# The products of the sample states with R~ | A~ made among the second layer's last gates, with their results in the sample's operand slots

## The chip, the cores and the metric

The kernel runs on one core of one Trainium2 chip. The metric is device time in microseconds (us) of one execution, the median of several runs. The engines of the core are TensorE (PE, with its weight loads as PEld), VectorE (DVE), ScalarE (ACT), GpSimd (POOL) and SyncE (SP, which issues most of the DMA transfers).

## The reference, cut to what matters

Two layers of a decoder trunk run over 1024 prompt tokens and over 8 sample sequences of 8 tokens each, 1088 tokens in all. Layer 0 mixes tokens with HGRN2, layer 1 with RWKV-7. Only layer 1 is touched. Its recurrence, for each of 16 heads of width 64, is

```
def step(S, inp):
    r_t, w_t, k_t, v_t, a_t, b_t = inp
    sa = jnp.einsum('bhij,bhj->bhi', S, a_t)
    S = S * w_t[:, :, None, :] + sa[..., None] * b_t[:, :, None, :] + v_t[..., None] * k_t[:, :, None, :]
    y = jnp.einsum('bhij,bhj->bhi', S, r_t)
    return S, y
```

The prompt starts from a zero state. Each of the 8 sample sequences starts from a state of its own, `state_rwkv` (8 x 16 x 64 x 64). Beside the mixer the layer has memory cross-attention and a gate of 1536 columns: the branch is multiplied by SiLU(gate) and projected back.

## The kernel before

Layer 1 is computed in blocks (class `Blk`): 8 of 128 prompt tokens and one, the sample block, of the 64 sample tokens; they run in the order of `RSEQ`, block 0, the sample block, block 1, 2 and so on. For a block, `pre` makes the decayed operands R~ and A~ (tile `AR`) and K~ and B~ (`BKz`); `score_steps` multiplies them to the matrix `Q` (products `psc`); `tokens` transposes `BKz` (`pbk`, `BKt`); `inverse` makes the inverses of the small triangular parts, mostly 30 short instructions on DVE, one after the other (`pd`, `Xc`), between `Ld`, `Lu` and `XN`, `XP`; `merge_steps` puts them together by many products of 32 x 32 on PE (`pn`, `px`, `py`). `chain` is the recurrence: PSUM tiles `chain0`, `chain1` and `chainS` begin with what the incoming state contributes, the first product by `Q` goes to `W` (ACT), the second to `UV` (DVE), the third gives the outputs `yv`.

For a prompt block, the incoming state is one matrix for all tokens. For the sample block it is 8 matrices for a pair of heads, and `sample_in` (line 1606) makes the product of each with its sequence's part of `AR`. It runs 8 times: for one pair of heads, 4 DMAs on SP bring the state (`Sn0`, rows of 256 bytes), PE transposes it into PSUM (line 1602, `ps`), ACT copies it out (`S0T`), PE makes 8 products for each of two heads (line 1617, `pas`, 16 columns each), and ACT copies each head's result into `AS0`. All of `ps` and `pas` go through one PSUM buffer (`psn`). `chain` of the sample block then adds `AS0` into `chain0` and `chain1` by products with the identity (line 1647). The sample block's chain comes second; `sample_in` stands ahead of the chain of the first (`SIN = 0`).

Ahead of the chains stand 12 gates. `gate(n)` loads 128 weight columns, multiplies them in three pieces of columns (384, 384, 320) with all 1088 tokens, 24 products a piece (72 rows of PE a gate, lines 216 to 218, into PSUM tiles `pg`), evacuates each piece by a DVE instruction (line 157), three ACT instructions (158 to 160) and a DVE product (line 1136), and sends the 544 KB of the gate (`evs`) to memory (`gT`). The three `pg` buffers hold the three pieces of one gate; the 5 slots of the ring `evslot` are given out in the order of the program. `PLAN` and `PLAN2` (line 43) set that order: cross-attention heads (x), the sample's cross-attention (s, products `pss`, `ppts`, `pos`, `pots`), gates (g) and the parts of the first two blocks. After `PLAN`, the PSUM of the cross-attention (`psx`) is closed and `psn` is opened in its place.

Within the order of the pools, a scheduler places each engine's instructions by times of its own. So the queues of the engines, which run in that order on the chip, are read from the built program.

Of the kernel before, what the change touches and what calls it, by code (L numbers as in the profile page):

```python
# [9 lines left out]
F32 = mybir.dt.float32  # L10
F32R = mybir.dt.float32r
I32 = mybir.dt.int32
AF = mybir.ActivationFunctionType
# [7 lines left out]
NB = 8  # L21
LS = 8
# [18 lines left out]

PARTS = dict(p="pre", c="score", t="tokens", i="inverse", m="merge")
PLAN, PLAN2 = [[(x[0], int(x[1:])) for x in l.split()] for l in (
    "x0 g0 x1 x2 g1 x3 g2 s0 g3 s1 g4 p0 c0 s2 g5 s3", "t0 i0 m0 p1 g6 g7 g8 g9 g10 g11")]
SIN = 0
EM = "sss"
ENG = dict(wm="gpsimd", um="gpsimd", vb="gpsimd", om="gpsimd", oa="gpsimd", bk0="gpsimd", bk1="vector", arA="gpsimd", arR="gpsimd", bx="vector", de="vector", ys="gpsimd", yr="vector", arC="gpsimd", sm="gpsimd", sa="vector", snm="vector", sna="vector", bkt="scalar", xm="scalar", ye="scalar")
# [925 lines left out]
def rwkv_layer(ctx, g, nn, left):  # L973
    nc, tc = g.nc, g.tc
# [70 lines left out]
    with pool(g, "lora", LB, "right") as lp:  # L1045
# [29 lines left out]
        for t0, n in PCS:  # L1075
# [3 lines left out]
            ps, pq = (g.psg.tile([128, 512], F32, name="pg", tag="g") for _ in range(2))  # L1079
            m = min(n, TP - t0)  # L1080
            smp = m < n
            for z, (wh, wl) in enumerate(l1):
                o, w = (pq, m) if z else (ps, n)
                for k in range(KT):
                    ks, x = slice(128 * k, 128 * k + 128), slice(t0, t0 + w)
                    for i, (a, v) in enumerate(((wh, xh), (wh, xl), (wl, xh))):
                        nc.tensor.matmul(o[:, :w], a[:, ks], v(k)[:, x], start=k + i == 0,
                                         stop=(k, i) == (KT - 1, 2) and (z == 1 or not smp))
# [98 lines left out]
    def gate(j, gemm=gemm_cm):  # L1187
        proj(3584, [j], xh, xl, g.gT, "silu", gemm=gemm, raws=1)
# [35 lines left out]
    for kind, n in PLAN2:  # L1224
        if kind == "g":
            gate(n)
        else:
            ops(n, PARTS[kind])
    es.close()

    with pool(g, "rl", 1, "right") as rl, pool(g, "sm2", 2, "right") as g.sm2:
# [19 lines left out]
        ops(2, "pre")  # L1251
        pairs = list(range(8))
        for n, x in enumerate(seq):
            if n == SIN:
                smp.sample_in()
            with tc.high_priority():
                x.chain()
            ops(n + 1, "values")
            weave(seq[n + 1].merge_steps() if n + 1 < len(seq) else (), seq[n + 2].score_steps() if n + 2 < len(seq) else (), *WV)
            ops(n + 2, "tokens", "inverse")  # L1260
            ops(n + 3, "pre")
            if n:
                seq[n - 1].out()
            if n > seq.index(smp) and pairs:
                smp.sample_out(pairs[:SOUT])
                pairs = pairs[SOUT:]
            if n == len(seq) - 2:
                pS.close()
                g.wp = ctx.enter_context(pool(g, "wp2", 2))
                owa, orb = ctx.enter_context(pool(g, "owA", 1)), ctx.enter_context(pool(g, "orb1", 1))  # L1270
                first = BranchTile(g, 1, orb, SEQ[0])
                first.load(KS)
                ws = load_out_w(g, 1, owa, [(g.wp, {})], KS[:OWB])
# [91 lines left out]
class Blk:  # L1365
# [22 lines left out]

    def pre(self):

        self.AR, self.ec = [], []
        for k in range(2):
            self.pre_group(k)

    def pre_group(self, k):
# [11 lines left out]
        k2 = ld(g.k2T, "k2")  # L1407
        a = self.at % 3
        AR = self.spare("AR", f"{('xhi', 'xlo')[k]}{4 + a}", 1024)
        AR = AR.rearrange("p (c e t) -> p c e t", c=4, t=64)  # L1410
        self.AR.append(AR)
        BK = g.BKz[k]
# [175 lines left out]
        for _ in self.merge_steps():  # L1588
            pass

    def sample_state(self, p):

        g = self.g
        nc = g.nc
        S0T = self.tile("S0T", "S0T", NB, 64)
        ps = g.psn.tile([128, NB, 64], F32, name="ps0", tag="n")
        for b0 in range(0, NB, 4):
            Sn0 = self.tile("Sn0", "Sn0", 4, 2, 64, p=64)
            for h in range(2):
                nc.sync.dma_start(out=Sn0[:, :, h, :], in_=g.state_rwkv[0, b0:b0 + 4, 2 * p + h].rearrange("b i j -> i b j"))  # L1600
            for bb in range(4):
                nc.tensor.transpose(ps[:, b0 + bb, :], Sn0[:, bb].rearrange("p h j -> p (h j)"), g.ident[:64, :64])
        nc.scalar.activation(S0T, ps, AF.Copy)
        return S0T

    def sample_in(self):

        g = self.g
        nc = g.nc
        self.AS0 = self.tile("AS0", "AS0", 4, 2, 128)  # L1610
        for p in range(8):
            S0T = self.sample_state(p)
            o = HV[p // 4]
            for h in range(2):
                ps = g.psn.tile([128, 2, NB, LS], F32, name="pas", tag="n")
                for bb in range(NB):
                    nc.tensor.matmul(ps[o, :, bb, :], S0T[HV[h], bb, :], self.AR[p // 4][HV[h], p % 4, :2, LS * bb:LS * bb + LS],  # L1617
                                     start=True, stop=True)
                nc.scalar.activation(self.AS0[o, p % 4, h], ps[o].rearrange("p a b t -> p (a b t)"), AF.Copy)

    def chain(self):

# [9 lines left out]
        for e in range(E):  # L1632
# [7 lines left out]
            def start(k):  # L1640
                G = Gs[k]
                if not self.sample and not S:
                    nc.tensor.matmul(G, g.zb, g.zb[:, None, :].to_broadcast([128, 4, 128]), start=True, stop=False)
                for j in range(4):
                    if self.sample:
                        for h in range(2):
                            nc.tensor.matmul(G[:, j, HV[h]], self.AS0[HV[k], j, h], g.ident[HV[k], HV[k]],
                                             start=j + h == 0, stop=False)
                    elif S:
                        nc.tensor.matmul(G[:, j], AR[k][:, j, 2 * e:2 * e + 2].rearrange("p a t -> p (a t)"), S[k][:, j],  # L1650
                                         start=j == 0, stop=False)
# [201 lines left out]
```

## Time and profile before

| | |
|---|---|
| runs of the kernel before | 2386.75, 2386.9, 2400.98 us |
| median | 2386.9 us |
| the profiled execution's own time | 2401.76 us |
| its span | 2399.8 us |
| PE busy | 2238.2 us (93%), 20980 instructions |
| DVE, ACT, POOL busy | 1332.2, 1004.3, 717.7 us |
| mean granted clock of PE | 0.934 of full speed |

The profiled execution is one like the slowest of the three runs. Times within it are counted from the span's start. The first layer and the projections of the second fill the span to about 1500 us, the cross-attention and the gates to 1745, the chains to about 2205, the output projection the rest. A line of a view names the engine, the line of the code, the result and its operands, the count, and in brackets how long the engine stood idle before, and what ended that.

### The profile page before, as it was taken

What the parts mean: (1) busy time and instruction counts of PE and PEld (TensorE: products, weight loads), DVE (VectorE), ACT (ScalarE), POOL (GpSimd) and SP (SyncE); (2) the same over time, 40 slices, a digit from 0 to 9 for tenths busy, and PEclk for the clock granted to TensorE, in tenths of its full rate; (3) what the DMA queues carried; (4) which work ended last, traced back from release to release, by engine and by line L of the source; (5) the groups of instructions that cost most, each with busy time, mean ns of one, the idle gap of its engine ahead of it and who ended that gap; (6) DMA issues with size and microseconds to landing.
All of it is one profiled execution on the core that took longest, in us unless ns stands there. A gap on an engine that the chain in (4) does not pass through costs nothing. (4 is left out here: it accounts for less than half of the span.)

```text
span 2399.8 us, 50625 instructions
## 1 busy us (share of the span) xinstructions
PE 2238.2 (93%) x20980; PEld 2001.5 (83%) x20981; DVE 1332.2 (56%) x2678; ACT 1004.3 (42%) x2240; POOL 717.7 (30%) x559
## 2 busy tenths in 40 slices
PE   5988999999999979989989998999999998899997
PEld 5988888888788858878979998898889987788786
DVE  6113566556775553365796214245576589874643
ACT  4222444444444442266554313344544455444421
POOL 2123121122112310034553412113143255444432
PEclk9998999999999989999999998999986798887999
DMA  5334111223432264215434425145332233312653
GB/s 184 86 96 142 48 56 45 67 70 91 111 87 87 80 193 127 84 41 199 148 122 163 127 93 145 50 103 134 113 108 72 57 101 99 90 55 82 201 158 105
DMA packets 360312, 252.99 MB, mean 105 GB/s; under 512 B 120379, under 2 KB 326403, under 8 KB 360083
## 3 DMA queue, kind: packets, MB, share of 16 engines
q1 hardware_dynamic: 348034, 237.66, 33.3%
q0 software_dynamic: 2544, 7.64, 0.9%
q10 hardware_dynamic: 9504, 4.46, 0.7%
q8 instruction: 165, 2.70, 0.5%
q14 instruction: 65, 0.52, 0.1%
HBM read 172.59 MB, written 77.11 MB: 104 GB/s over the span
## 5 line engine op out<-in xcount | busy, mean ns | idle before, releaser
L200 POOL TENSOR_TENSOR wlo<-wraw,whi 128x1024 fp32r<-128x1024 f32 (+1 forms) x84 | 214.9, 2560 | 646.5 <-ACT whi L197 623.8
L216 PE MATMUL pg<-hi,whi 128*128 128x288 f32 (+3 forms) x800 | 269.1, 336 | 4.5 <-DVE qk L597 2.3
L218 PE MATMUL pg<-hi,wlo 128*128 128x288 f32 (+3 forms) x800 | 266.0, 333 | 0.0
L217 PE MATMUL pg<-lo,whi 128*128 128x288 f32 (+3 forms) x800 | 265.9, 332 | 0.0
L197 ACT ACTIVATE whi<-wraw 128x1024 fp32r<-128x1024 f32 (+1 forms) x92 | 101.0, 1099 | 178.5 <-issue 104.9
L216 PEld LDWEIGHTS pg<-hi,whi 128*128 128x128 f32 x800 | 153.8, 192 | 21.5 <-issue 4.4
L217 PEld LDWEIGHTS pg<-lo,whi 128*128 128x128 f32 x800 | 153.7, 192 | 12.9 <-issue 3.1
L218 PEld LDWEIGHTS pg<-hi,wlo 128*128 128x128 f32 x800 | 153.5, 192 | 11.8 <-issue 2.3
L890 PE MATMUL pout<-owh,bh 128*128 128x512 f32 (+1 forms) x432 | 143.1, 397 | 9.2 <-ACT owh L197 9.2
L890 PE MATMUL pout<-owl,bh 128*128 128x512 f32 (+1 forms) x432 | 142.0, 394 | 0.1
L890 PE MATMUL pout<-owh,bl 128*128 128x512 f32 (+1 forms) x432 | 141.2, 394 | 0.9 <-DVE bl L200 0.9
L216 PE MATMUL pg<-xhi,whi 128*128 128x384 f32 (+2 forms) x392 | 127.6, 325 | 7.1 <-DVE evs L1136 5.0
L218 PE MATMUL pg<-xhi,wlo 128*128 128x384 f32 (+2 forms) x392 | 126.4, 322 | 0.0
L217 PE MATMUL pg<-xlo,whi 128*128 128x384 f32 (+2 forms) x392 | 125.5, 320 | 0.0
L1461 PE MATMUL psc<-AR,BKz 128*128 128x128 f32 x544 | 98.2, 342 | 17.2 <-DVE Q L1464 9.3
L1461 PEld LDWEIGHTS psc<-AR,BKz 128*128 128x128 f32 x544 | 86.7, 244 | 23.1 <-DVE Q L1464 11.0
L890 PEld LDWEIGHTS pout<-owh,bh 128*128 128x128 f32 (+1 forms) x432 | 78.9, 183 | 31.3 <-ACT owh L197 10.8
L197 ACT ACTIVATE bh<-br 128x512 fp32r<-128x512 f32 (+1 forms) x54 | 32.4, 606 | 171.5 <-POOL br L859 84.4
L200 DVE TENSOR_TENSOR bl<-br,bh 128x512 fp32r<-128x512 f32 (+1 forms) x54 | 49.6, 919 | 96.2 <-ACT bh L197 96.2
L890 PEld LDWEIGHTS pout<-owh,bl 128*128 128x128 f32 (+1 forms) x432 | 78.6, 182 | 22.8 <-DVE bl L200 1.8
L242 PE MATMUL pg<-xhi,wlo 128*128 128x384 f32 (+1 forms) x408 | 96.6, 334 | 0.0
L890 PEld LDWEIGHTS pout<-owl,bh 128*128 128x128 f32 (+1 forms) x432 | 78.8, 183 | 21.1 <-DVE owl L200 0.6
(460 smaller groups left out, 6114.9 us busy)
## 6 DMA issues: line engine op xcount, KB each, us to landing
wraw<-in_w_in_dram SPq DMA_DIRECT2D x72, 512.0 KB
oraw<-in_w_out_dram SPq DMA_DIRECT2D x24, 512.0 KB
wraw<-in_w_mem_kv_dram SPq DMA_DIRECT2D x16, 512.0 KB
gT<-evs SPq DMA_DIRECT2D x12, 544.0 KB
vv<-vtk SPq DMA_DIRECT2D x24, 256.0 KB
br<-brT SPq DMA_DIRECT2D x24, 256.0 KB
br<-mixT SPq DMA_DIRECT2D x24, 256.0 KB
gt<-gT SPq DMA_DIRECT2D x24, 256.0 KB
```

The source lines that it names most:

```text
L197: nc.scalar.activation(hi, src, AF.Copy)
L200: (nc.gpsimd if elo == "pool" else nc.vector).tensor_sub(lo, src, hi.bitcast(F32))
L216: nc.tensor.matmul(out, ah, bh, start=first, stop=False)
L217: nc.tensor.matmul(out, ah, bl, start=False, stop=False)
L218: nc.tensor.matmul(out, al, bh, start=False, stop=last)
L242: nc.tensor.matmul(z[:, :n], a[:, k], x(k)[:, t0:t0 + n], start=first, stop=last)
L890: nc.tensor.matmul(ps[c][:p], a[:, k, :p], w[:, 512 * c:512 * c + 512], start=first, stop=last)
L1461: nc.tensor.matmul(ps[:, j], two(BK[:, h, j, 2 * e:2 * e + 2]), two(AR[:, j, 2 * e:2 * e + 2]), start=True, stop=True)
```

## The change

`sample_in` and `sample_state` take one pair of heads as an argument and are no longer called ahead of the first chain. `PLAN2` gets eight items a0 to a7, two behind each of the gates 6 to 9, which call them. The state and its transpose (`Sn0`, `S0T`) take slots of `evslot`, and the results go into the upper halves of the two spare slots in which the sample's `AR` uses the lower halves only. Nothing is computed otherwise.

```diff
 PLAN, PLAN2 = [[(x[0], int(x[1:])) for x in l.split()] for l in (
-    "x0 g0 x1 x2 g1 x3 g2 s0 g3 s1 g4 p0 c0 s2 g5 s3", "t0 i0 m0 p1 g6 g7 g8 g9 g10 g11")]
+    "x0 g0 x1 x2 g1 x3 g2 s0 g3 s1 g4 p0 c0 s2 g5 s3", "t0 i0 m0 p1 g6 a0 a1 g7 a2 a3 g8 a4 a5 g9 a6 a7 g10 g11")]
...
     for kind, n in PLAN2:
         if kind == "g":
             gate(n)
+        elif kind == "a":
+            smp.sample_in(n, evslot)
...
         for n, x in enumerate(seq):
-            if n == SIN:
-                smp.sample_in()
             with tc.high_priority():
                 x.chain()
...
         AR = self.spare("AR", f"{('xhi', 'xlo')[k]}{4 + a}", 1024)
+        if self.sample:
+
+            self.AS0.append(AR[:, 512:].rearrange("p (c h t) -> p c h t", c=2, h=2))
+            AR = AR[:, :512]
...
-    def sample_state(self, p):
+    def sample_state(self, p, slot_):
...
-        S0T = self.tile("S0T", "S0T", NB, 64)
+        S0T = slot_("S0T")[:, :512].rearrange("p (b i) -> p b i", b=NB)
+        Sn = slot_("Sn0")[:64, :1024].rearrange("p (a b h j) -> p a b h j", a=2, b=4, h=2)
...
-            Sn0 = self.tile("Sn0", "Sn0", 4, 2, 64, p=64)
+            Sn0 = Sn[:, b0 // 4]
...
-    def sample_in(self):
+    def sample_in(self, p, slot_):
...
-            nc.scalar.activation(self.AS0[o, p % 4, h], ps[o].rearrange("p a b t -> p (a b t)"), AF.Copy)
+            nc.scalar.activation(self.AS0[j // 2][o, j % 2, h], ps[o].rearrange("p a b t -> p (a b t)"), AF.Copy)
...
-                            nc.tensor.matmul(G[:, j, HV[h]], self.AS0[HV[k], j, h], g.ident[HV[k], HV[k]],
+                            nc.tensor.matmul(G[:, j, HV[h]], self.AS0[j // 2][HV[k], j % 2, h], g.ident[HV[k], HV[k]],
```

Lines behind the changed ones stand 2 to 4 lines further down (157, 216 to 218 and 1136 keep theirs; 1602 is 1607 now, 1617 is 1620, 1619 is 1622, 1652 is 1655).

The first place is PE at the end of the sample's cross-attention, around its last two softmaxes. Before:

```order
L216 MATMUL pg<-xhi,whi 128x384
L217 MATMUL pg<-xlo,whi 128x384
L425 MATMUL pots<-ident,oS 128x128
L218 MATMUL pg<-xhi,wlo 128x384
L216 MATMUL pg<-xhi,whi 128x384
L217 MATMUL pg<-xlo,whi 128x384
```

Of the change (the gate row at its end is the first of gate 8; 288 gate rows are still to come there):

```order
L415 MATMUL pos<-xlo,PTs 32x128 x16
L402 MATMUL pss<-kcT,qs 32x256 x8
L408 MATMUL ppts<-ident,prob 128x128 x4
L415 MATMUL pos<-xlo,PTs 32x128 x16
L425 MATMUL pots<-ident,oS 128x128
L1607 MATMUL ps_17672<-ident,Sn_17671 128x64 x8
L1620 MATMUL pas<-AR,S0T 64x2x8 x8
L1493 MATMUL pbk<-ident,BKz_15166 128x64 x16
L1620 MATMUL pas<-AR,S0T 64x2x8 x8
L1465 MATMUL psc<-AR,BKz_15165 128x128 x8
L1607 MATMUL ps_17708<-ident,Sn_17707 128x64 x8
L1620 MATMUL pas<-AR,S0T 64x2x8 x8
```

Before, gate rows stand between all the steps of the cross-attention and behind it: at `pots` 190 of the rows of gates 6 to 11 are still to come. Now none stand between the last `pss` and gate 8, and 98 more are left for later.

The second place is DVE, where gate 7 is evacuated. Its three pieces are `pg_17677`, `pg_17707` and `pg_17737` before, ahead of the last softmax:

```order
L157 TENSOR_SCALAR evs_17676<-pg_17677 128x384
L326 TENSOR_SCALAR nm_16926<-mx_16924 128x2
L332 RECIPROCAL ri_16931<-smx_16928 128x2
L334 TENSOR_TENSOR ri_16931<-ri_16931,bmask_122 128x2
L336 TENSOR_SCALAR prob_16923<-prob_16923,ri_16931 128x256 x2
L1136 TENSOR_TENSOR evs_17676<-pg_17677,evs_17676 128x384
L157 TENSOR_SCALAR evs_17676<-pg_17707 128x384
L1136 TENSOR_TENSOR evs_17676<-pg_17707,evs_17676 128x384
L157 TENSOR_SCALAR evs_17676<-pg_17737 128x320
L1136 TENSOR_TENSOR evs_17676<-pg_17737,evs_17676 128x320
```

They are `pg_17749`, `pg_17779` and `pg_17809` with the change:

```order
L1538 TENSOR_TENSOR pd_17227<-Xc_15171,L16_17225 128x14x14
L157 TENSOR_SCALAR evs_17748<-pg_17749 128x384
L1539 TENSOR_REDUCE Xc_15171<-pd_17227 128x14
L157 TENSOR_SCALAR evs_17748<-pg_17779 128x384
L157 TENSOR_SCALAR evs_17748<-pg_17809 128x320
L1538 TENSOR_TENSOR pd_17227<-Xc_15171,L16_17225 128x15x15
L1539 TENSOR_REDUCE Xc_15171<-pd_17227 128x15
L1136 TENSOR_TENSOR evs_17748<-pg_17749,evs_17748 128x384
L1545 STREAM_TRANSPOSE XN_17261<-XI_17258 128x16x2x16
L1546 STREAM_TRANSPOSE XP_17262<-XI_17258 128x16x2x16
L1136 TENSOR_TENSOR evs_17748<-pg_17779,evs_17748 128x384
L1136 TENSOR_TENSOR evs_17748<-pg_17809,evs_17748 128x320
```

Gate 7's evacuation now stands in the last steps of block 0's inverse; until then its pieces hold all three `pg` buffers.

The third place is ACT, at the evacuation of gates that run behind block 0's merge. Before, a piece's three instructions (here of gate 11) follow each other:

```order
L158 ACTIVATE evs_18068<-evs_18068 128x384
L159 ACTIVATE evs_18068<-evs_18068 128x384
L160 ACTIVATE evs_18068<-evs_18068 128x384
L1295 ACTIVATE XM_17265<-px32_17338 32x512
L1295 ACTIVATE XM_17265<-px32_17339 32x512
L158 ACTIVATE evs_18068<-evs_18068 128x384
```

With the change (gate 9, and the copies of a4 and a5):

```order
L1608 ACTIVATE S0T_18010<-ps0_18012 128x512
L1622 ACTIVATE AR_17532<-pas_18026 64x128
L1622 ACTIVATE AR_17532<-pas_18036 64x128
L197 ACTIVATE whi_18350<-wraw_18352 128x1024
L1608 ACTIVATE S0T_18046<-ps0_18048 128x512
L158 ACTIVATE evs_18088<-evs_18088 128x384 x2
L159 ACTIVATE evs_18088<-evs_18088 128x384
L158 ACTIVATE evs_18088<-evs_18088 128x320
L1622 ACTIVATE AR_17532<-pas_18062 64x128
L159 ACTIVATE evs_18088<-evs_18088 128x384
L160 ACTIVATE evs_18088<-evs_18088 128x384
```

All of gate 9's sigmoids now stand behind a5's copy `S0T_18046`, whose source PE makes only behind the last row of gate 9.

## Rows read from the trace of the kernel before

**Rows 1.** The page, part 2: clock of PE in 40 slices, tenths
```profile
PEclk9998999999999989999999998999986798887999
```

**Rows 2.** Windows: stretch, length, busy PE, PEld, DVE, ACT, POOL (count); clock, DMA
```profile
1755.00:1790.00 35.00, 32.59 (x432) 30.11 (x432) 31.62 (x60) 14.27 (x33) 19.35 (x22) 0.94 0.41 111
1790.00:1832.00 42.00, 42.00 (x424) 39.24 (x423) 25.50 (x54) 17.94 (x43) 14.65 (x11) 0.52 0.24 64
1832.00:1846.00 14.00, 14.00 (x255) 13.05 (x254) 9.92 (x13) 9.80 (x25) 3.39 (x3) 0.93 0.31 76
1846.00:1894.00 48.00, 48.00 (x552) 45.08 (x551) 20.22 (x46) 17.52 (x42) 6.96 (x6) 0.50 0.25 62
```

**Rows 3.** Timeline of PE: start, duration, engine, line, tiles, count [idle before]
```profile
1678.21 1.08 PE L415 MATMUL pos<-xlo,PTs 128*32 128x128 f32 x32
...
1710.23 0.69 PE L216 MATMUL pg<-xhi,whi 128*128 128x384 f32 x1 [3.54 <-DVE evs L1136]
...
1723.62 1.20 PE L1560 MATMUL pn<-XN,Q 32*32 32x32 f32 x64
...
1751.13 3.78 PE L1461 MATMUL psc<-AR,BKz 128*128 128x128 f32 x16
...
1754.85 2.15 PE L1652 MATMUL chain<-UV,Q 128*64 128x64 f32 x32
```

**Rows 4.** Tile windows of PE: `pas`, then `ps`: length, busy (rows), clock, DMA
```profile
1754.00:1790.00 36.00, 4.58 (x64) 0.93 0.42 113
1790.00:1890.00 100.00, 21.05 (x192) 0.57 0.24 62
...
1754.00:1790.00 36.00, 2.69 (x24) 0.93 0.42 113
1790.00:1890.00 100.00, 4.83 (x42) 0.57 0.24 62
```

**Rows 5.** Timeline of DVE, from the last softmax to the inverse's end
```profile
1680.22 0.69 DVE L324 TENSOR_REDUCE mx<-pss 128x2 f32<-128x512 f32 x1 [0.57 <-PE pss L402]
...
1683.15 0.62 DVE L336 TENSOR_SCALAR prob<-prob,ri 128x256 f32<-128x256 f32 x2
...
1696.28 0.28 DVE L426 COPY os<-pots 128x128 f32<-128x128 f32 x1
...
1700.58 0.70 DVE L1528 STREAM_TRANSPOSE Lu<-Ld 128x512 f32<-128x512 f32 x1
...
1720.47 1.12 DVE L1541 STREAM_TRANSPOSE XN<-XI 128x512 f32<-128x512 f32 x1 [0.52 <-ACT XI L1538]
```

**Rows 6.** Source view of `Ld`: ns min/median/max, first and last start
```profile
L1525 ACT ACTIVATE Ld<-Q,bm x16: 483/510/532, 1692.8 to 1698.9; 32x128 f32<-32x128 f32 x16
```

**Rows 7.** Groups of DVE, 1700 to 1723 us: count | busy, mean ns | idle before
```profile
L1534 DVE TENSOR_TENSOR pd<-Xc,L 128x1 f32<-128x1 f32 (+14 forms) x15 | 5.4, 361 | 0.4
L1535 DVE TENSOR_REDUCE Xc<-pd 128x1 f32<-128x1 f32 (+14 forms) x15 | 3.6, 239 | 0.4
L1415 DVE TENSOR_TENSOR_SCAN G<-smask,sg 128x512 f32<-128x512 bf16 x1 | 3.3, 3326 | 0.0
L157 DVE TENSOR_SCALAR evs<-pg 128x384 f32<-128x384 f32 (+1 forms) x4 | 2.1, 532 | 5.0 <-PE pg L218 5.0
...
L1425 DVE TENSOR_TENSOR BKz<-bb,sg 64x256 f32<-64x256 f32 x2 | 1.4, 702 | 0.0
```

**Rows 8.** Tile window of PE: gate rows, length, busy (rows), clock
```profile
1676.00:1706.00 30.00, 24.64 (x145) 1.00 0.45 135
```

**Rows 9.** ACT: a group of the gates' sigmoids, 1676 to 1755; the first `S0T`
```profile
L158 ACT ACTIVATE evs<-evs 128x384 f32<-128x384 f32 (+1 forms) x13 | 6.5, 501 | 18.6 <-DVE evs L157 18.6
...
1759.13 0.60 ACT L1603 ACTIVATE S0T<-ps 128x512 f32<-128x512 f32 x1
```

**Rows 10.** Timelines of SP and DVE behind the last gate row
```profile
1744.52 0.32 SPq L1141 DMA_DIRECT2D gT<-evs  x1
...
1747.92 1.29 DVE L1464 TENSOR_TENSOR Q<-psc,rms 128x512 f32<-128x512 f32 x2 [3.43 <-DMA UV<-vtk]
```

More of the change, by code (lines that the diff above doesn't have):

```diff
@@ L1389, in pre @@
     def pre(self):
-        self.AR, self.ec = [], []
+        self.AR, self.ec, self.AS0 = [], [], []
         for k in range(2):
@@ L1604, in sample_state @@
         return S0T
-    def sample_in(self):
+    def sample_in(self, p, slot_):
         g = self.g
         nc = g.nc
[L1610 to L1618, printed above, removed]
-                nc.scalar.activation(self.AS0[o, p % 4, h], ps[o].rearrange("p a b t -> p (a b t)"), AF.Copy)
+        S0T = self.sample_state(p, slot_)
+        o, j = HV[p // 4], p % 4
+        for h in range(2):
+            ps = g.psn.tile([128, 2, NB, LS], F32, name="pas", tag="n")
+            for bb in range(NB):
+                nc.tensor.matmul(ps[o, :, bb, :], S0T[HV[h], bb, :], self.AR[p // 4][HV[h], j, :2, LS * bb:LS * bb + LS],
+                                 start=True, stop=True)
+            nc.scalar.activation(self.AS0[j // 2][o, j % 2, h], ps[o].rearrange("p a b t -> p (a b t)"), AF.Copy)
     def chain(self):
```

## The prediction

> **What bounds the kernel now.** I read the page first, for PE's clock: it is nearly full everywhere but in two or three slices around 1800 to 1900 us, where the chains begin [rows 1]. The windows then split that stage. From 1755 to 1790 DVE is busy 31.62 of 35 us and PE 32.59, both nearly full at a clock of 0.94. From 1790 to 1894 PE has no idle time at all (42.00 of 42, 14.00 of 14, 48.00 of 48), and 90 of these 104 us run at about 0.5, which is the 1.2 GHz level [rows 2]. So there PE alone is the bound, and any row taken from it shortens the stage. `pas` and `ps` belong to that stage: 4.58 + 2.69 us of them lie before 1790, 21.05 + 4.83 us behind it [rows 4].
>
> Ahead of it, the timelines of PE and DVE and the source view of `Ld` give a string of dependences: last softmax, last `os`, `Ld`, `Lu`, the inverse on DVE, `XN`, the merge (`pn`), the first `chain` product at 1754.85 [rows 3, 5, 6]. In the kernel before, PE fills the waits of this string with gate rows, 145 of them between 1676 and 1706 at 24.64/145 = 0.17 us a row [rows 8]. The one visible wait of a gate row is 3.54 us at 1710.23, for gate 7's evacuation [rows 3].
>
> **What is removed.** Nothing is computed less. The rows of `pas` and `ps` leave the chain stage. Behind 1790 they are 21.05 + 4.83 = 25.9 us of a busy PE: I count all of it as gained there. Before 1790 I count nothing of the 7.27 us, since DVE's 31.62 of 35 us stays; the bounds are 0 and 3.4 us, DVE's idle share. The copies on ACT leave too (0.60 us for an `S0T` [rows 9]); ACT is busy 14.27 of 35 there [rows 2], so they are worth nothing.
>
> **What is added among the gates.** At full clock a `pas` row costs 4.58/64 = 0.072 us and a `ps` row 2.69/24 = 0.112 us [rows 4], so the 256 and 66 rows are 18.3 + 7.4 = 25.7 us. If they only lengthened PE's work there, the change would exchange 25.9 for 25.7. What decides is therefore whether PE has waits there that they fill, or whether new waits come. I follow the string.
>
> *The last softmax.* Thirteen gate rows less stand ahead of the second-last `pos`, 13 x 0.17 = 2.2 us, so the last `mx` comes at 1678.0 for 1680.22. From `mx` to the end of `prob` it is 3.6 us [rows 5]; the transposes, `pos` (1.08 us [rows 3]), `pots` and `os` (0.28 [rows 5]) take some 3.4 more with no gate row in between. `os` is done at about 1685 for 1696.56: 11.5 us earlier, but PE stands idle for about 4.6 us of it, which the gates filled.
>
> *The inverse.* The 16 `Ld` take 6.6 us from 1692.8 to 1699.4 [rows 6]; `Lu` moves from 1700.58 to about 1691. From `Lu` to `XN` it was 19.9 us [rows 5]. What DVE must do in it: `pd` 5.4, `Xc` 3.6, the scan `G` 3.3, `BKz` 1.4, three of gate 7's L157 1.6, `Lu` 0.7 [rows 5, 7], together 16.0, and about 3.3 of small instructions and gaps. That is 19.3, so `XN` comes at about 1710.3 for 1720.47. In this stretch PE has only a0, a1, `pbk` and the first `psc`: gate 8's first row waits until gate 7's first L1136 has been done, and that stands behind the last `Xc`. So PE is idle from about 1697 to 1709, 11 or 12 us. This is the new wait, and its counterpart before was 3.54 us.
>
> *The merge.* `pn` came 3.15 us behind `XN`, and the first `chain` 3.7 us behind the `psc` at 1751.13 that closes the stretch [rows 3]. So `pn` is at 1713.4 for 1723.62. From `pn` to that `psc` it was 27.5 us; with fewer gate rows but a2 and a3 in between I take 28.5, to 1741.9.
>
> *What is left then.* Before, the last gate row had run by this time. Now the 216 rows of gates 9 to 11 are left, 216 x 0.17 = 36.7 us, and a4 to a7, half of the sample's rows: 9.2 + 3.6 = 12.8 us. Together, to 1791.4. On ACT, the sigmoids of gates 9 and 10 stand behind `S0T` of a5 and a7, whose source PE makes only behind the gate's last row; so the `pg` buffers come free late, and the first row of gates 10 and 11 waits for a `S0T`, three ACT instructions (0.501 us each [rows 9]) and DVE's two. The trace has no such wait. Below it is 0 (if the sigmoids' times allow the three buffers to turn), above 6 us, two pieces' evacuations; the nearest row is the 3.54 us [rows 3], and I take 3.2 each: 1797.8.
>
> *The last gate.* Behind its last row come an L157 (0.53), three of ACT (1.5), an L1136 (0.5), the `gT` transfer, and then the load of `UV` from the memory side: from the issue at 1744.52 to the `Q` that waited for it at 1747.92 are 3.4 us [rows 7, 9, 10]. That is 6.1 us during which PE has nothing, since all else of the two blocks is done. Before, 3.78 us of `psc` and parts of the merge covered it [rows 3]. The first `chain` starts at about 1803.9 for 1754.85: **49 us later**.
>
> **The sum.** 49 - 25.9 = +23 us against the profiled execution's own 2401.76, so 2425. That execution lies 14.9 us above the median, 2386.9, and no row says where the shorter runs gain; the likeliest place is the stretch at half clock, the only large part of the trace whose length could change with no instruction changed. There, less of the 25.9 us would be saved. A version whose PE idles so often before the chains will not lack half-clock stretches either. I take half of the 14.9: **2417 us**, +1.3% against the median. About 1% (24 us) is what a measurement of this kernel can tell from no change.
>
> **The rivals.**
> 1. *The forecast*: the wait before gate 8, the late gates and the lost cover of the last evacuation outweigh the gain, the clock stays as it is: 2408 to 2432. Chance 0.45.
> 2. *The clock*: the stage runs at full clock once the sample's small rows have left it. Its 100 us of PE behind 1790 become 45 to 50, DVE's 25.50 + 9.92 + most of 20.22 us [rows 2] then set about 58. That is -42 for -25.9, so +7 against the profile, 2409, or 2395 to 2412. For it: ahead of the first fall, around 1790, PE is not full (32.59 of 35). Against it: at 1846 the clock falls with PE busy 14.00 of 14 and 48.00 of 48 on the two sides [rows 2]. Chance 0.18. The Trainium skill (TensorE: Matmul & The Clock Gate, Part 1: The HAM clock gate) says that the throttled clock is the default, that sustained activity of PE releases it and idleness brings it back; by this rule a stage without idle time would be at the full level. The trace disagrees: PE is busy 48.00 of 48.00 us at 0.50 [rows 2], so the rule gets this smaller chance.
> 3. *The stalls are half as long*: DVE reaches gate 7's L1136 earlier, or the `S0T` don't hold the sigmoids. 6 us less before gate 8 and 6 us less at gates 10 and 11 give a chain start of +37 and a sum of +11 on the profile; against the median with shorter half-clock stretches, 2388 to 2404. Chance 0.15.
> 4. *The other side*: the inverse, now 10 us earlier, is done before PE runs out of work, and the sample's rows take the place of the 3.54 us wait. Then the chain starts only 25.7 - 3.5 = 22 us later, and with rival 2's stage (-42) the time is 20 us below: 2367 to 2382 as profile or run goes. It decides itself at gate 8's first row: PE idle under 3 us there and `pn` by 1705. Against it: DVE's 19.3 us of its own work between `Lu` and `XN`. Chance 0.09.
> 5. *Worse*: the idle stretches bring half the clock into the first 35 us of the chains too. PE's 32.59 - 7.27 = 25.3 us there become about 48, 13 more than the 35: 2430 to 2440. The waits for the last gate, 6.1 us with nothing for PE just ahead of the chains, speak for it. Chance 0.13.
>
> **How the numbers follow.** 2417 is the first case. The range leaves out 4 and the upper half of 5, some 0.15: 2388 to 2434. Faster by over 1% means under 2363: only the tail of 4, 0.03. Slower by over 1%, above 2411: seven eighths of the first case, all of 5 and the tip of 2, 0.54. The rest, 0.43 (2 and 3, most of 4, an eighth of the first), is within 1%.
>
> **What would show it.** In the profile after: PE idle some 4 to 5 us around 1686 and some 11 us before gate 8's first row, which waits for DVE's `evs` of L1136; `XN` near 1710 and `pn` near 1713; waits of about 3 us for ACT or DVE at the first rows of gates 10 and 11; 72 rows of gate 11 alone, about 6 us of idle PE, and the first `chain` near 1804; no `pas` behind it; the stretch between there and block 1's chain shorter by about 26 us, at half clock again. I would be wrong if PE's idle time before gate 8 is small, if the gates' rows run under the inverse after all, or if the chain stage's clock is full or much worse: the last moves the time by 17 to 40 us and no order of instructions shows it.

## The result and the profile after

The changed kernel takes 2423.4 us (median of 4 runs, 2420.4 to 2431.2) against 2393.3 us for the kernel before (4 runs, 2386.8 to 2401.0): a ratio of 1.013, interval 1.0082 to 1.0177, so about 30 us slower. In the runs of the experiments below the kernel before had a median of 2393 to 2395, with single runs from 2380 to 2407. The profiled execution of the change took 2422.14 us, near its median; that of before was one of the longer runs (2401.76).

To compare the two traces, one row serves as a mark: the last transpose of the cross-attention's heads (`ppt`), ahead of everything that the change moves. The source view gives for a line its operation, the count, the shortest, median and longest ns, and the first and the last start. Before:

```profile
L350 PE MATMUL ppt<-ident,prob x128: 270/272/473, 265.7 to 1619.9; 128*128 128x128 f32 x128
L1652 PE MATMUL chain<-UV,Q x544: 221/222/369, 1754.8 to 2225.3; 128*64 128x64 f32 x182
```

After:

```profile
L350 PE MATMUL ppt<-ident,prob x128: 270/272/477, 266.2 to 1614.9; 128*128 128x128 f32 x128
L1655 PE MATMUL chain<-UV,Q x544: 222/222/370, 1805.4 to 2247.6; 128*64 128x64 f32 x182
```

The mark comes 5.0 us earlier in the trace of after, for reasons that lie ahead of the change; all times of after below are to be read with these 5.0 us added before they are held against the prediction's. From the mark to the first chain product it was 134.9 us and is 190.5, **55.6 longer**. From the first chain product to the start of the last one by `UV` it was 470.5 us and is 442.2, **28.3 shorter**. I call the second "the chains' part". 55.6 - 28.3 - 5.0 and -1.9 behind the chains make +20.4 between the two profiles. Each part is read from one execution of each kernel.

PE's timeline of after shows the place (start, duration, line, count, idle before and what ended it):

```profile
1677.11 0.70 PE L408 MATMUL ppts<-ident,prob 128*128 128x128 f32 x4 [3.57 <-DVE prob L336]
...
1681.70 1.11 PE L1607 MATMUL ps<-ident,Sn 64*128 64x64 f32 x8 [0.39 <-DVE os L426]
1685.69 1.86 PE L1620 MATMUL pas<-AR,S0T 64*64 64x16 f32 x16 [2.88 <-ACT S0T L1608]
...
1701.52 0.69 PE L216 MATMUL pg<-xhi,whi 128*128 128x384 f32 x1 [4.48 <-DVE evs L1136]
...
1706.92 1.20 PE L1564 MATMUL pn<-XN,Q 32*32 32x32 f32 x64
...
1731.98 1.89 PE L1620 MATMUL pas<-AR,S0T 64*64 64x16 f32 x16
...
1738.97 0.69 PE L216 MATMUL pg<-xhi,whi 128*128 128x384 f32 x1
...
1742.55 0.34 PE L218 MATMUL pg<-xhi,wlo 128*128 128x384 f32 x1
...
1757.60 1.10 PE L1620 MATMUL pas<-AR,S0T 64*64 64x16 f32 x16 [0.98 <-ACT S0T L1608]
1759.49 1.89 PE L1620 MATMUL pas<-AR,S0T 64*64 64x16 f32 x16 [0.79 <-ACT AR L1622]
...
1771.91 1.10 PE L1620 MATMUL pas<-AR,S0T 64*64 64x16 f32 x16
...
1783.76 0.69 PE L216 MATMUL pg<-xhi,whi 128*128 128x384 f32 x1 [0.81 <-DVE evs L1136]
...
1799.16 0.39 PE L1646 MATMUL chain<-zb 128*128 128x512 bf16 x1 [1.93 <-DVE zb L1245]
...
1800.55 3.60 PE L1465 MATMUL psc<-AR,BKz 128*128 128x128 f32 x16 [0.22 <-DVE Q L1468]
1805.43 2.18 PE L1655 MATMUL chain<-UV,Q 128*64 128x64 f32 x32 [1.28 <-POOL UV L1505]
```

ACT's `Ld`, DVE around gate 8's first row, and POOL ahead of the first chain product:

```profile
1678.47 6.45 ACT L1529 ACTIVATE Ld<-Q,bm 32x128 f32<-32x128 f32 x16
...
1684.96 0.71 DVE L1532 STREAM_TRANSPOSE Lu<-Ld 128x512 f32<-128x512 f32 x1 [3.31 <-ACT Ld L1529]
...
1700.91 0.56 DVE L1136 TENSOR_TENSOR evs<-pg,evs 128x384 f32<-128x384 f32 x1 [0.17 <-ACT evs L160]
1702.12 1.10 DVE L1545 STREAM_TRANSPOSE XN<-XI 128x512 f32<-128x512 f32 x1 [0.65 <-ACT XI L1542]
...
1803.35 1.56 POOL L1659 MEMSET W<- 64x512 f32 x3 [4.56 <-DMA UV<-vtk]
1804.86 3.53 POOL L1505 MEMSET UV<- 64x512 f32 x7
```

The windows by stage, with columns as in [rows 2] (length, busy PE, PEld, DVE, ACT, POOL with counts, clock, DMA): first the stretch from gate 7's last row to the first chain product, then two parts of its third window (the merge, and the end of the merge alone), then the beginning of the chains.

```profile
1671.00:1681.70 10.70, 5.65 (x90) 3.67 (x88) 3.24 (x9) 5.86 (x14) 3.21 (x3) 0.81 0.45 147
1681.70:1701.50 19.80, 11.78 (x96) 10.96 (x96) 13.06 (x39) 11.11 (x26) 4.83 (x6) 0.59 0.45 110
1701.50:1738.97 37.47, 37.45 (x616) 35.84 (x616) 8.09 (x13) 14.90 (x38) 2.54 (x2) 0.77 0.21 58
1738.97:1797.30 58.33, 54.57 (x377) 51.68 (x376) 9.97 (x20) 16.70 (x39) 2.55 (x2) 0.88 0.16 47
1797.30:1805.43 8.13, 4.36 (x18) 3.52 (x18) 5.69 (x12) 3.50 (x8) 3.45 (x6) 0.79 0.69 222
...
1706.92:1738.97 32.05, 32.05 (x596) 30.72 (x594) 5.24 (x9) 13.02 (x32) 2.35 (x1) 0.79 0.16 39
1727.00:1739.00 12.00, 12.00 (x182) 11.62 (x179) 0.75 (x2) 7.71 (x19) 0.00 (x0) 0.50 0.25 63
...
1805.00:1841.00 36.00, 31.72 (x417) 29.29 (x418) 31.47 (x58) 12.70 (x26) 23.94 (x30) 1.00 0.43 116
1841.00:1881.00 40.00, 36.71 (x444) 34.30 (x443) 34.27 (x62) 22.12 (x53) 23.75 (x21) 0.66 0.34 94
1881.00:1921.00 40.00, 34.54 (x560) 33.12 (x560) 35.25 (x80) 20.09 (x55) 14.69 (x12) 0.69 0.28 77
```

PE is idle for 5.0, 8.0, 0.0, 3.8 and 3.8 us in the first five, and its clock is under 0.9 in all of them, where before it was 1.00 between 1676 and 1706 [rows 8]. Before, PE was not idle in the first 18 us of the merge either, at the full clock:

```profile
1723.60:1741.80 18.20, 18.20 (x335) 17.33 (x335) 7.10 (x12) 7.76 (x17) 0.10 (x1) 1.00 0.13 48
```

At the beginning of the chains PE is no longer busy all the time as in [rows 2]: 36.71 and 34.54 of 40, DVE 34 to 35, at a clock of 0.66 to 0.69.

The same columns for the two whole parts, first from the mark to the first chain product (before, after), then the chains' part (before, after):

```profile
1619.90:1754.85 134.95, 125.03 (x1279) 116.97 (x1277) 71.16 (x142) 63.26 (x146) 35.91 (x38) 0.94 0.45 126
1614.90:1805.43 190.53, 164.63 (x1598) 152.22 (x1595) 70.05 (x143) 71.55 (x172) 32.85 (x31) 0.85 0.36 99
...
1754.85:2225.30 470.45, 444.44 (x6798) 403.34 (x6799) 341.90 (x651) 220.17 (x550) 215.06 (x214) 0.81 0.30 83
1805.43:2247.60 442.17, 406.04 (x6477) 366.34 (x6479) 340.96 (x651) 212.06 (x526) 222.66 (x223) 0.81 0.31 85
```

Ahead of the chains PE's busy time grew by 39.6 us and its idle time by 16.0. In the chains' part its busy time fell by 38.4 us and its idle time grew by 10.1.

### The profile page after: what moved, and what is told of

It reads as the page before. It is cut to its first block, busy times and chain, and to the rows that moved or that the text cites. A ratio compares the mean times of both kernels' runs of the same rounds, so it can differ in the third digit from the quotient of the medians.

```text
span 2420.4 us, 50634 instructions
## 1 busy us (share of the span) xinstructions
PE 2237.5 (92%) x20980; PEld 1998.3 (83%) x20981; DVE 1326.3 (55%) x2678; ACT 1003.2 (41%) x2240; POOL 718.9 (30%) x559
## 5 line engine op out<-in xcount | busy, mean ns | idle before, releaser
L216 PEld LDWEIGHTS pg<-hi,whi 128*128 128x128 f32 x800 | 152.8, 191 | 21.4 <-issue 4.1
L1465 PE MATMUL psc<-AR,BKz 128*128 128x128 f32 x544 | 92.9, 331 | 17.0 <-DVE Q L1468 9.4
L890 PEld LDWEIGHTS pout<-owh,bl 128*128 128x128 f32 (+1 forms) x432 | 78.9, 183 | 21.4 <-issue 0.4
```

Of the source, the lines that this page charges most:

```text
L216: nc.tensor.matmul(out, ah, bh, start=first, stop=False)
L890: nc.tensor.matmul(ps[c][:p], a[:, k, :p], w[:, 512 * c:512 * c + 512], start=first, stop=last)
L1465: nc.tensor.matmul(ps[:, j], two(BK[:, h, j, 2 * e:2 * e + 2]), two(AR[:, j, 2 * e:2 * e + 2]), start=True, stop=True)
```

## The experiments

All kernels stand in one table. "To the chains" is from the mark to the first chain product, "chains' part" as above, both in the profiled execution; the difference of medians is against the kernel before in the same runs. The ratio with its 95% interval is not the quotient of the two medians, so the two can differ by 0.1 to 0.2%.

| kernel | median us | difference | ratio, interval | to the chains | chains' part |
|---|---|---|---|---|---|
| before | 2393.3 | | 1 | 134.9 | 470.5 |
| the change | 2423.4 | +30.1 | 1.0130 (1.0082 to 1.0177) | 190.5 | 442.2 |
| none | 2364.0 | -29.4 | 0.9868 (0.9823 to 0.9913) | 135.9 | 442.0 |
| layout | 2401.8 | +8.3 | 1.0044 (1.0025 to 1.0063) | 137.2 | 462.9 |
| own | 2397.7 | +4.3 | 1.0007 (0.9991 to 1.0024) | 148.1 | 453.0 |
| late | 2394.8 | +1.4 | 1.0000 (0.9980 to 1.0021) | 185.8 | 417.2 |
| thin | 2410.3 | +16.2 | 1.0061 (1.0038 to 1.0084) | 173.0 | 442.4 |
| mid | 2422.5 | +28.4 | 1.0112 (1.0085 to 1.0139) | 181.1 | 446.6 |
| own_early | 2391.6 | -2.5 | 0.9990 (0.9966 to 1.0015) | 158.4 | 430.8 |
| own_two | 2400.0 | +5.9 | 1.0025 (1.0007 to 1.0044) | 157.7 | 452.4 |
| shift | 2372.0 | -23.0 | 0.9900 (0.9860 to 0.9939) | 141.9 | 437.4 |
| late_two | 2416.5 | +21.4 | 1.0078 (1.0051 to 1.0105) | 183.0 | 435.0 |
| own_high | 2405.9 | +10.9 | 1.0056 (1.0026 to 1.0085) | 150.6 | 446.6 |

**none: the price of the products in their old place.** From the kernel before:

```diff
     def sample_in(self):
         self.AS0 = self.tile("AS0", "AS0", 4, 2, 128)
-        for p in range(8):
-            ...
+        self.g.nc.gpsimd.memset(self.AS0, 0.0)
```

> The kernel before without the 8 products of the sample states (ps, pas and their copies are left out, the sample's AS0 is set to zero). It prices the products in the place where they stood. Theory (they are PE rows in a stage that PE bounds at half clock): the first chain product stands where it did, the time from there is 26 to 33 us shorter, so about 30 us less than before. Rival (the small rows are what takes the clock away): the stage runs at full clock, 42 us less or more. Rival (they were hidden behind DVE): less than 10 us.

29.4 us less, with the chains beginning where they did and their part 28.5 us shorter: the theory. The products are worth 29 us among the chains, and the stage is not at full clock without them:

```profile
1753.60:1790.00 36.40, 33.77 (x393) 30.80 (x392) 32.43 (x63) 12.43 (x27) 19.45 (x21) 0.92 0.32 88
1790.00:1830.00 40.00, 37.19 (x478) 35.08 (x476) 34.67 (x66) 21.95 (x50) 23.84 (x19) 0.73 0.35 91
1830.00:1870.00 40.00, 28.99 (x454) 26.63 (x455) 34.91 (x72) 19.88 (x58) 19.79 (x17) 0.61 0.29 81
```

Without them DVE is the busier engine, 34.67 and 34.91 of 40 us, and the clock still falls to 0.73 and 0.61. The rival that the small rows take the clock away has fallen here. No `pas` row of the change stands behind its first chain product, and the chains' part is 442 in `none` and in the change. So by these two profiles the loss of 59 us against `none` lies ahead of the chains (54.6 there).

**layout: the place of the results alone.** The products ahead of the first chain as before (`PLAN2` without a0 to a7), with tiles of their own and only the results in the halves of `AR`:

```diff
+            if n == SIN:
+                for p in range(8):
+                    smp.sample_in(p, None)
...
-        S0T = slot_("S0T")[:, :512].rearrange("p (b i) -> p b i", b=NB)
+        S0T = self.tile("S0T", "S0T", NB, 64)
```

> The products stay ahead of the first chain as before, with tiles of their own; only their results go into the free halves of AR, as in the change. Theory: no difference, within 5 us of before; all of the change's loss is in where the products stand. Rival (the results in AR bind the chain to the whole slot, or its next block to it): 5 us or more slower.

8.3 us slower by the medians, 0.25 to 0.63% by the ratio: the expectation was missed by 3 us, and by its number the rival (5 us or more) holds. The scheduler places some `pas` and `psc` of the chains in another order, and its profile shows the chains' part shorter, not longer, than in the profile of before; from which of its parts the 8 us come I cannot show. Whether the place of the results binds the chains, as the rival had it, is not shown. `own`, below, has its results in the same place and is 4.3 us above before, so this is at most a small part of the 30 us.

**own: the ring taken out.** The plan of the change, but the states and transposes in two spare slots that the third block in the order uses later:

```diff
+    smp.sslots = [smp.spare(nm, nm + "6", 1024) for nm in ("xhi", "xlo")]
...
-        S0T = slot_("S0T")[:, :512].rearrange("p (b i) -> p b i", b=NB)
-        Sn = slot_("Sn0")[:64, :1024].rearrange("p (a b h j) -> p a b h j", a=2, b=4, h=2)
+        S0T = self.sslots[0][:, 512 * (p % 2):512 * (p % 2) + 512].rearrange("p (b i) -> p b i", b=NB)
+        Sn = self.sslots[1][:64, :1024].rearrange("p (a b h j) -> p a b h j", a=2, b=4, h=2)
```

> The plan of the change, but the states and their transposes take two free slots of their own instead of slots of the ring that the gates use, so that the gates keep the order of before and stand under the cross-attention and the inverse again. Theory (the ring is what pushed 98 gate rows behind the merge and uncovered the waits): gate 8's wait is near 3.5 us, the gates end some 10 to 20 us later than before for the products between them, the chains' part is 15 to 25 us shorter; 2380 to 2395, about like before, 30 us less than with the change. Rival (the products themselves, at their clock, cost it, wherever they stand among the gates): 2410 to 2425.

2397.7, 26 us less than the change, and no difference from before by its interval; 3 us above the upper end that I had set. The chains begin 13.2 us later than before and their part is 17.5 shorter, both as expected. The gate rows stand under the cross-attention and the inverse again; the gate row that waits there (now gate 10's first) waits 1.93 us:

```profile
1709.04 1.10 PE L1621 MATMUL pas<-AR,xhi 64*64 64x16 f32 x16
...
1713.02 0.45 PE L216 MATMUL pg<-xhi,whi 128*128 128x384 f32 x1 [1.93 <-DVE evs L1136]
```

Its `pas` rows, ahead of the first chain product and behind it:

```profile
1622.70:1770.80 148.10, 10.70 (x144) 0.95 0.44 119
1770.80:1870.00 99.20, 11.03 (x112) 0.76 0.33 86
```

144 rows run among the gates, 112 are left for the chains, at 0.074 and 0.098 us a row. So `own` differs from the change in two ways, the ring and these 112 rows. But with the rows of `ps` the products cost PE 28.2 us in `own` and 28.2 in the change, so the 26 us between the two kernels are not rows of the products. They come with the order that the shared ring gives the gates; the products themselves cost about as much among the gates as among the chains.

**thin: the ring kept, the rows taken out.** From the change:

```diff
-            for bb in range(NB):
-                nc.tensor.matmul(ps[o, :, bb, :], S0T[HV[h], bb, :], self.AR[p // 4][HV[h], j, :2, LS * bb:LS * bb + LS],
-                                 start=True, stop=True)
+            nc.tensor.matmul(ps[o].rearrange("p a b t -> p a (b t)"), S0T[HV[h], 0, :], self.AR[p // 4][HV[h], j, :2, :],
+                             start=True, stop=True)
```

> The kernel with the change, but each head's 8 small products are one product of 128 columns with the first sequence's state (so the other sequences' states are left out): 16 products instead of 128, while the ring, the transposes, the DMAs, the copies and the wait for the PSUM buffer stay. The products' rows cost 21.7 us of PE in the changed kernel, 1 to 3 us here. Theory (of the 59 us that the change adds to the kernel without the products some 26 are the ring's order and the waits, the rest the rows): 2398 to 2408, so 34 to 44 us remain above the kernel without the products. Rival (the rows alone, at their clock): 2370 to 2380. Rival (the order alone): above 2412.

2410.3, 46 us above `none` and 13 below the change; the theory's range ended at 2408. The 16 products cost more than I had put down, and the difference to the change's rows (tile windows of `pas`, the change first, then thin) is close to the 13 us:

```profile
1600.00:2000.00 400.00, 21.69 (x256) 0.84 0.35 95
...
1600.00:2000.00 400.00, 8.11 (x32) 0.85 0.37 100
```

21.69 - 8.11 = 13.6. On the way to the chains alone the two profiles differ by more, 17.5 us, so as far as these two executions tell some 4 us of waits went with the rows. As an estimate, the 59 us are 21.7 (`pas`) + 6.5 (`ps`, by its tile window) = 28 of rows and about 30 of the order around them. `own` gives nearly the same for the order (26).

**late: all items behind gate 11.**

```diff
-"t0 i0 m0 p1 g6 a0 a1 g7 a2 a3 g8 a4 a5 g9 a6 a7 g10 g11"
+"t0 i0 m0 p1 g6 g7 g8 g9 g10 g11 a0 a1 a2 a3 a4 a5 a6 a7"
```

> The ring stays shared, but all eight items stand behind gate 11, so gates 6 to 11 are as before and the products run behind the last gate, one pair after the other through the one PSUM buffer. Theory: gates as before; some 6 pairs of about 5 us each stand between the merge and the chains, covering the 6 us of the last gate's transfer, the chains start 25 to 30 us later and end 26 to 33 us sooner from there: 2385 to 2400. Rival (products outside the chains cost as much as in the change): 2415 to 2425.

The time is as the theory had it, 2394.8, but not by its numbers. The chains begin 50 us later than in `none`, not 25 to 30: behind the merge the pairs run alone, each 6.3 us, at a granted clock of 0.50:

```profile
1778.41 1.11 PE L1607 MATMUL ps<-ident,Sn 64*128 64x64 f32 x8 [0.36 <-ACT AR L1622]
1780.21 1.89 PE L1620 MATMUL pas<-AR,S0T 64*64 64x16 f32 x16 [0.69 <-ACT S0T L1608]
1782.45 1.89 PE L1620 MATMUL pas<-AR,S0T 64*64 64x16 f32 x16 [0.36 <-ACT AR L1622]
1784.70 1.11 PE L1607 MATMUL ps<-ident,Sn 64*128 64x64 f32 x8 [0.36 <-ACT AR L1622]
...
1760.00:1803.00 43.00, 33.40 (x277) 30.69 (x277) 1.89 (x3) 7.99 (x22) 0.00 (x0) 0.50 0.25 62
```

16 `pas` rows take 1.89 us here and 1.10 between gate rows (the change at 1771.91). What brings the time down is a chains' part of 417 us, 25 less than in `none`, with nearly the same number of rows and no product of the sample in either. The windows of the whole part, `late` and then `none`:

```profile
1807.00:2224.20 417.20, 386.13 (x6480) 347.81 (x6480) 338.55 (x651) 211.88 (x526) 225.13 (x219) 0.87 0.32 87
...
1753.60:2195.60 442.00, 411.43 (x6525) 368.51 (x6524) 346.83 (x655) 214.69 (x528) 223.04 (x219) 0.84 0.31 83
```

PE's idle time is 31 us in both. All of the difference is busy time, 25.3 us, at a mean clock of 0.87 against 0.84. So the theory's time came out by two misses that cancelled, the way to the chains 20 us or more too long and the chains' part 25 us shorter than `none`'s.

**mid: all items between gates 9 and 10.**

```diff
-"t0 i0 m0 p1 g6 a0 a1 g7 a2 a3 g8 a4 a5 g9 a6 a7 g10 g11"
+"t0 i0 m0 p1 g6 g7 g8 g9 a0 a1 a2 a3 a4 a5 a6 a7 g10 g11"
```

> The ring shared as in the change, but all eight items stand between gate 9 and gate 10, so gates 6 to 9 keep their places and only gates 10 and 11 come behind the products. Theory (what counts is how many gate rows are taken out from under the cross-attention and the inverse): gate 8's wait as before, 72 to 144 gate rows behind the merge; slower than with all items at the end (2395), faster than the change (2423): 2400 to 2415. Rival (any sharing costs the whole): 2420 or more.

2422.5, as slow as the change: the theory fell, since it counted gate rows only. The gate row that waits under the inverse waits 2.74 us, and just gate 11's 72 rows are left behind the merge, but most of the pairs again have no gate rows to run with (from 1745 to 1779.5 PE runs at 0.50), and the last gate has nothing behind it:

```profile
1777.77 1.89 PE L1620 MATMUL pas<-AR,S0T 64*64 64x16 f32 x16 [0.42 <-ACT AR L1622]
1779.59 0.69 PE L216 MATMUL pg<-xhi,whi 128*128 128x384 f32 x1
...
1801.40 2.18 PE L1655 MATMUL chain<-UV,Q 128*64 128x64 f32 x32 [1.11 <-POOL UV L1505]
```

**own_early, own_two, own_high: can it beat the kernel before?** The first is `own` with the sample's operands made first and the products right behind the cross-attention (block 0's `tokens` then reads the sample's `BKz`, so block 0's outputs are not the reference's):

```diff
-"t0 i0 m0 p1 g6 a0 a1 g7 a2 a3 g8 a4 a5 g9 a6 a7 g10 g11"
+"p1 t0 i0 a0 a1 a2 a3 a4 a5 m0 a6 a7 g6 g7 g8 g9 g10 g11"
```

The second is the same with the transposes in the inverse's PSUM buffers:

```diff
-        ps = g.psn.tile([128, NB, 64], F32, name="ps0", tag="n")
+        ps = g.psi.tile([128, NB, 64], F32, name="ps0", tag="i")
```

The third is `own` with

```diff
-            smp.sample_in(n)
+            with tc.high_priority():
+                smp.sample_in(n)
```

> Slots of their own as in the run before this one, and the sample block's operands made first, so that the products come right behind the cross-attention, one between every 20 gate rows. Theory (between gate rows the products run at full clock, 25.7 us for all, and leave the chains wholly): first chain product 18 to 24 us later than without the products, chains as without them: 2382 to 2392, 2 to 10 us faster than before. Rival (the merge comes later for them, or the chains keep a low clock anyway): 2395 to 2405.

> As the run before, with the transposes through the inverse's two PSUM buffers instead of the products' one, so that a pair does not wait for the copy of the last. Theory: as the run before or up to 6 us faster, 2378 to 2390. Rival (the inverse's merge now waits for these buffers): its first product comes 10 us or more later than in the run before, 2390 to 2402.

> Slots of their own, the products with the priority of the chains: two of the eight pairs are left when the first chain starts. Theory (at full clock between gate rows the products cost 25.7 us, against 29 in the chains, and PE's 3.5 us of waits under the inverse are filled): 2384 to 2394, between no difference and 9 us faster than before. Rival (the chains' part loses what the gates gain): 2394 to 2402.

None of them is faster than before by more than its interval: -2.5, +5.9 and +10.9 us. `own_early` ends at the upper edge of the theory's range, `own_two` in that of its rival, whose condition is met too (`pn` comes 118.3 us behind the mark, 102.3 in `own_early`), `own_high` above both of its ranges. In the profiles they exchange 16 to 24 us ahead of the chains for 18 to 40 in their part, against a profile of before that is one of its longer runs; and single runs of `own_high` lie between 2388 and 2419 us and its profiled one is the shortest, so that its row of the table flatters it.

**late_two: a pair without the wait for the single buffer.** `late` with the edit of `own_two`:

```diff
-        ps = g.psn.tile([128, NB, 64], F32, name="ps0", tag="n")
+        ps = g.psi.tile([128, NB, 64], F32, name="ps0", tag="i")
```

> All items behind gate 11, as in the earlier run, but the transposes go through the inverse's two PSUM buffers, so that a pair's transposes don't wait for the copy of the last. Theory (a pair takes 6.3 us there, of which 1.1 wait for the copy of the transposes and 0.7 for the copies of the results): 1 to 2 us less for each of 8 pairs, 8 to 14 us sooner at the first chain product, and 2380 to 2390. Rival (the half clock alone sets it): within 4 us of the earlier run, 2391 to 2399.

Neither held: 2416.5. The way to the chains became 2.8 us shorter, not 8 to 14, because the transposes now begin only when the merge has left the inverse's buffers (the first 133.1 us behind the mark, in `late` 125.8). The chains' part went from 417 to 435 us, some 7 of it busy time of PE and 10 idle time, though no instruction of it was touched on purpose.

**shift: does the chains' part hang on when it begins?** `none` with 40 rows of zeros ahead of the first chain:

```diff
-                    nc.tensor.matmul(G, g.zb, g.zb[:, None, :].to_broadcast([128, 4, 128]), start=True, stop=False)
+                    for d in range(40 * (1 - k) + 1):
+                        nc.tensor.matmul(G, g.zb, g.zb[:, None, :].to_broadcast([128, 4, 128]), start=d == 0, stop=False)
```

> The kernel without the products (their part of the result is left out), with 40 more rows of zeros times zeros (128x512, bfloat16) ahead of the first chain, so that the chains start 6 to 15 us later and right behind wide rows, with nothing else changed by intention. Between the kernels so far the chains' part, from the first chain product on, took 442 us in three kernels and 417 in the one with all items behind the last gate, by busy time of PE at a lower clock and not by its waits. Theory (the chains' part is set by their instructions): the chains start 6 to 15 us later, their part stays within 5 us of 442, 2368 to 2380. Rival (it hangs on how the chains meet the clock): their part changes by 10 us or more, to one side or the other.

The way to the chains is 6.0 us longer, their part 4.6 shorter, the median 8 us above `none`: the theory. A start 6 us later did not bring `late`'s 25 us; one as late as `late`'s was not tried.

## Why the prediction was right

It forecast 2417 and slower; it was 2423.4. Its two terms were +49 ahead of the chains and -25.9 within; measured were +55.6 and -28.3, and by the medians of `none` +59 and -29.4. Step by step, with 5.0 us added to the times of after:

- **The gain in the chains** was right in place and nearly in size, the size in part by luck. 25.9 counted only the rows behind 1790 and nothing before, and the experiment without the products gives 28.5 to 29.4. But the stage did not stay one that PE alone bounds, at half clock: PE's busy time there fell by 38.4 us (the rows of `pas` and `ps` were 33.1), and 10.1 us of that came back as idle time.
- **The last softmax and the inverse.** PE's first idle stretch, due to be 4.6 us, was 5.0. `Lu` was due at 1691 and came at 1690.0; `XN` at 1710.3 and came at 1707.1; `pn` at 1713.4 and came at 1711.9. One link of the string was read wrongly: `Ld` does not wait for `os`. It begins at 1678.47, ahead of `os` (1681.36), and before too it began first (1692.8 [rows 6], `os` at 1696.28 [rows 5]), behind a gate's sigmoids on ACT. `Lu` came when it was due because `os` and `Ld` moved by nearly as much. The inverse was 2.1 us shorter (17.2 us from `Lu` to `XN` for 19.3). Its largest gain is the scan `G`, 1.23 us and not the 3.3 of [rows 7]; smaller gains of `pd` and `BKz` were taken back by waits.
- **The wait before gate 8** (whose counterpart before, 3.54 us in [rows 3], is one of gate 10's first row for gate 9's evacuation, 144 rows being left behind it, and not for gate 7's as I wrote) was there, for the same instruction (L1136), but 4.48 us and not 11 to 12. I had let the products of a0 and a1 run at full clock; they and the first `psc` ran at 0.59, waited 3.6 us for copies, and filled the time. PE's idle time from the last `os` to gate 8 is 8.0 us.
- **The merge** was due to take 28.5 us and took 32.1 (from `pn` to gate 9's first row at 1738.97). PE had no idle time in it: the clock was 0.79. Gate 8's last row ran at 1721.79; behind it the rest of the merge, the last products of a2 and those of a3 ran with no gate rows in between, at 0.50 from 1727 to 1739. Before, with gate rows in between, the merge's first 18 us ran at 1.00. This step failed by what I had left out, a clock below the full one ahead of the chains.
- **The 216 gate rows and a4 to a7** were due to take 49.5 us and 6.4 us of waits. The rows took 54.57, at a clock of 0.88, and the waits 3.8 in all; of these 1.8 stand ahead of gate 10's first row and 1.9 ahead of gate 11's, for 3.2 each. Most of it is the products' own wait for their copies on ACT; gate 11's first row itself waited 0.81 us. The order of the sigmoids behind `S0T` was real, the stall priced for it was about half as long.
- **The last gate** was left uncovered as forecast, 8.13 us from its last row to the first chain product for 6.1. PE was not without work in it (4.36 us, most of it a `psc`), and the load of `UV` took the 3.4 us that were forecast; what I had left out are POOL's MEMSETs of `W` and `UV` behind that load, 2.1 us.

So the waits were overestimated by some 8 us (20.6 in the five windows, for about 29), and PE's work ahead of the chains was underestimated by some 15, mostly the clock. The errors cancelled in part: the chains began 6.5 us later than they were due. That the sum is so near is partly luck. PE's busy time from the mark to the first chain product rose from 125.03 to 164.63 us, 39.6, of which `pas` and `ps` are 28.2 and dearer rows of other products 11.4; its idle time there rose by 16.0. (The 66 rows of `ps` in the prediction are 64; that changes its sum by 0.2 us.)

**The median.** I took half of 14.9 us off because the profiled execution of before was one of the longer. In more runs the median of before was 7 to 8 us below it. Without this term the sum was 2425, nearer to the 2423.4 that were measured. That the difference lies in the half-clock stretch alone is not borne out: the mark itself stands between 1611.5 and 1622.7 us in the traces of this study, so a part of what sets runs apart arises ahead of everything that was changed.

**The rivals.** The clock (2) fell: without the products the chains' beginning runs at 0.61 to 0.73 behind its first 36 us, in two kernels. (Its 58 us of DVE are more than the 55.6 that its three terms add up to.) The rule of the Trainium skill (TensorE: Matmul & The Clock Gate, Part 1: The HAM clock gate) that sustained activity of PE releases the throttled clock is not borne out here: in the change PE was busy 12.00 of 12.00 us at 0.50 at the end of the merge. The halved stalls (3) were right on the wait before gate 8, nearly right on those at gates 10 and 11, and wrong on the sum. The other side (4) fails at its own condition: gate 8's wait was 4.48 us, and `pn` came at 1711.9. That half the clock comes into the first 35 us of the chains (5) is not seen: the changed kernel's clock is 1.00 from 1805 to 1841.

**What stays open.** The chains' part is 417 to 447 us in seven kernels that have no product of the sample behind the first chain product; waits differ little between `late` and `none`, busy time at the granted clock does. Over all seven PE's idle time differs too, from 31 us (`none`, `late`) to 46 (`mid`). Which property of the order sets the clock there was not found: a shift by 6 us did not bring it. As each part is from one execution, and single runs of one kernel lie up to 31 us apart, differences of a few us between these parts show nothing.

## What to carry to other kernels

A task that borrows slots of another's ring takes its place in the ring's order too: ask which of the other's instructions can no longer be moved ahead of it, and what they used to cover. Here 98 gate rows left the places where PE would wait, and the order that came of it cost about as much as the moved products. But counting the rows that lose their place is not enough: `mid` left gates 6 to 9 where they were and lost as much, since most of its products then ran without gate rows beside them, at half clock. Moving work off a busy engine's stage gains nothing when the same engine is busy at the new place; here 29 us were taken out of the chains, and 28 came back as rows among the gates.

## What the runs showed of the hardware

The same `pas` rows take 1.10 us per 16 between gate rows (1771.91) and 1.89 in the merge behind the last row of gate 8 (1731.98), where PE is never idle and the granted clock is 0.50. The first gate rows behind such a stretch are at the lower level too: 0.52 us each from 1739.46 on, 0.34 from 1742.55. And a chains' part of like instructions varies by up to 25 us in PE's busy time between kernels whose change lies ahead of it (386.13 in `late`, 411.43 in `none`), which is nearly as much as the change under study moved; a small gain here can only be judged by several runs.
